# Strassen's scheme for the FFN output projections of a one-layer streaming block on Trainium2

## The chip, the cores and the metric

The kernel runs on one core of one Trainium2 chip. The metric is the device time of one execution in microseconds (us); the time of a kernel is the median of its runs. Engines are named as the profile names them: PE is TensorE, DVE is VectorE, ACT is ScalarE, SP is SyncE, whose queue issues the weight loads, and POOL is GpSimd. Each engine works through its own instruction queue in order, and semaphores tie the queues together.

## The reference

The kernel computes one layer of a post-norm block on 256 tokens of width 2048, all in float32:

```python
D_MODEL = 2048; SEQ = 256; D_FF = 5504; ALPHA = 2 ** 0.25

def swiglu_ffn(x, w_in, w_out):
    g, u = jnp.split(x @ w_in, 2, axis=-1)
    return (jax.nn.silu(g) * u) @ w_out

h = layer_norm(ALPHA * h + 0.5 * swiglu_ffn(h, ffn1_w_in, ffn1_w_out), ...)
h = layer_norm(ALPHA * h + hybrid_mixer(h, ...), ...)
h = layer_norm(ALPHA * h + memory_cross_attention(h, mem, ...), ...)
h = layer_norm(ALPHA * h + 0.5 * swiglu_ffn(h, ffn2_w_in, ffn2_w_out), ...)
```

Only the two FFNs matter here. The input projection is 256 x 2048 by 2048 x 11008 (gate and up halves of 5504 columns each), the output projection 256 x 5504 by 5504 x 2048.

## The kernel before

**Three passes for a float32 product.** TensorE multiplies in a reduced format (fp32r), so each operand is split into hi, the value rounded to that format (a CAST on ACT), and lo, the rest (a subtraction on DVE); `split` does both. A product is taken in three passes, hi·hi, lo·hi and hi·lo, which add up in a PSUM bank. Each matmul has a 128 x 128 block of activations as its stationary operand and 512 columns of weights as its moving one. The 256 tokens are two token tiles of 128.

**Loads.** Weights are read once, 1 MB at a time: a raw tile of 128 partitions x 2048 floats, from a pool of three. For the input projection a load holds two K-tiles (128 rows of the weight each) by 512 columns of the up and 512 of the gate matrix. Its two halves of 1024 columns are split into "units" (hi and lo tiles, four of each). A load is worth 2 K-tiles x 2 token tiles x 2 matrices x 3 passes = 24 matmuls. The function `run` walks a list of work items and, ahead of each, emits the DMA and the splits of loads further down the list, up to two ahead and as long as units are free; a scheduler (the Tile framework) then orders each engine's queue by the program's order, priorities (`SOON` is earlier) and its own estimate of times, and gives each tile a buffer that has come free.

**Groups.** `in_group` computes 512 gate and 512 up columns for all 256 tokens in eight loads, into four PSUM banks. `hidden` then gives two steps: `product` (silu of the gate times the up, on ACT and DVE) and `turn`, eight transposes on PE that bring the hidden block into the layout of a stationary operand, followed by a split of the turned tile from its PSUM bank (CAST on ACT, subtraction on DVE). The turn is woven in behind the second load of the next group. Banks come from two pools of four, `mm` and `at`, and consecutive groups alternate between them.

**Strassen's scheme.** Two K-tiles by two token tiles of activations are a 2 x 2 block matrix, and so are two K-tiles by two column halves of weights. In two of a group's eight loads (`SUMS_AT`, the loads 2 and 5) `mm_sums` takes the product of these by Winograd's form of Strassen's scheme: 7 block products instead of 8, hence 21 matmuls. It needs four sums of weight blocks and four of activation blocks. The weight sums are formed by `load_sums`: three additions on DVE in place in the raw tile (L177, L178), then two splits of 1024 columns into blocks that the tags X2 and X3 or H4 and H5 name. The activation sums are formed once for an FFN by `sum_forms`. Four of the seven products go into banks of the pool that the next group will use; `shared` combines them on ACT and DVE into four tiles (`w`, five buffers) that `product` adds.

**Parts and the output projection.** The hidden width is 43 K-tiles of 128. The FFN is done in three parts of 12, 16 and 15 K-tiles (`F_SPLIT`): the groups of a part, then `out_proj`, which multiplies the turned hidden tiles (blocks H0 to H3) by four K-tiles x 512 columns of output weights a load, all four column blocks in turn, plain (24 matmuls a load), and adds the bank to the residual h. The last turn of a part is woven in behind the second load of this projection.

## Time and profile before

| what | value |
| --- | --- |
| median of 3 runs | 2561.83 us (2561.34 to 2567.68) |
| profiled execution | 2568.53 us |
| its span, first to last instruction | 2566.8 us |
| granted PE clock | 0.998 |
| PE busy | 2548.4 us, 99% of the span |
| DVE busy | 1745.4 us, 68% |
| ACT busy | 1242.6 us, 48% |
| first FFN, with its layer norm | 0 to 642 us |
| mixer and cross attention | 642 to 1894 us |
| second FFN and the last layer norm | 1894 to 2567 us |

A row of the profile names the line of the kernel, the engine, the operation, the tile written and the tiles read (buffer numbers are left out), the shape, and how many instructions it stands for. In the timeline the first two numbers are the start and the duration in us, and a bracket at the end tells how long the engine was idle before it and what released it. In the table of stretches each engine has its busy time and its count of instructions; the last three numbers are the granted clock, the share of DMA time and GB/s. PEld is the load of a stationary operand, which overlaps the matmuls. T is the tile of the layer's input in its turned form, hi and lo the weight units, raw the loaded weights, X and H the blocks, w the tiles of 512 columns, ident the identity matrix of the transposes, mm and at PSUM banks.

### The profile page before, as it was taken

To read this page: it belongs to the slowest core of one execution; us is meant where nothing else is said; L and a number is where in the kernel's file an instruction comes from. 1 tells how busy PE (TensorE), PEld (TensorE's weight loads), DVE (VectorE), ACT (ScalarE), POOL (GpSimd) and SP (SyncE) were. 2 spreads that over 40 slices of the span, in tenths; PEclk is the share of its full clock that TensorE was granted. 3 is DMA by queue.
4 is the path that set the end of the run, shared out by engine and by line. 5 is a ranking of instruction groups with operands and counts; after the bars stand their busy time and mean duration, and the time that the engine had idled before them with its cause. 6 is when DMAs were issued, how large, how long until landed. Compare 5 with 4: busy or idle time off the path is not lost.

```text
span 2566.8 us, 31977 instructions
## 1 busy us (share of the span) xinstructions
PE 2548.4 (99%) x12652; PEld 2145.3 (84%) x12652; DVE 1745.4 (68%) x2317; ACT 1242.6 (48%) x1676; POOL 29.9 (1%) x87
## 2 busy tenths in 40 slices
PE   9999999999999999999999999999999999999998
PEld 8888888889888888888888888888888888888896
DVE  6857775776676776555657785555887578747856
ACT  5534553444454555544444564454554355434542
POOL 0000000000000000000000000000000000000000
PEclk9999999999999999999999999999999999999999
DMA  6655455555655642455556565543555555555563
GB/s 246 231 200 197 181 201 194 195 197 192 228 178 182 199 140 102 145 181 188 188 191 254 182 218 193 195 163 136 214 178 211 186 191 197 197 197 196 181 224 136
DMA packets 74038, 488.04 MB, mean 190 GB/s; under 512 B 8608, under 2 KB 8864, under 8 KB 20768
## 3 DMA queue, kind: packets, MB, share of 16 engines
q1 hardware_dynamic: 69216, 468.18, 50.8%
q0 software_dynamic: 3808, 15.73, 2.0%
q8 instruction: 99, 1.62, 0.2%
q10 hardware_dynamic: 864, 2.10, 0.2%
q14 instruction: 51, 0.42, 0.0%
HBM read 482.69 MB, written 2.10 MB: 189 GB/s over the span
## 4 chain that ended last, share of the span: by engine, by line
PE 95%; DVE 3%; DMA 1%; ACT 1%; issue 0%; DVEq 0%; ACTq 0%
PE mm L269 31%; PE mm L249 17%; PE mm L280 14%; PE at L280 12%; PE mm L250 8%; PE mm L325 3%; PE at L325 3%; PE mm L238 2%; PE at L814 1%; PE at L697 1%; PE at L844 1%; DVE lo L199 1%; PE at L1114 0%; DVE X L229 0%; DVE raw L178 0%; PE at L1092 0%
## 5 line engine op out<-in xcount | busy, mean ns | idle before, releaser
L199 DVE TENSOR_TENSOR lo<-raw,hi 128x1024 fp32r<-128x1024 f32 (+2 forms) x778 | 934.2, 1208 | 569.4 <-ACT hi L196 557.6
L196 ACT CAST hi<-raw 128x1024 fp32r<-128x1024 f32 (+2 forms) x778 | 807.3, 1041 | 850.9 <-PE mm L269 383.8
L269 PE MATMUL mm<-hi,H 128*128 128x512 f32 x1640 | 508.9, 390 | 1.9 <-ACT H L228 1.6
L249 PE MATMUL mm<-T,hi 128*128 128x512 f32 x1168 | 415.1, 399 | 0.0
L269 PEld LDWEIGHTS mm<-hi,H 128*128 128x128 f32 x1640 | 307.7, 188 | 66.8 <-ACT H L228 2.4
L280 PE MATMUL mm<-hi,T 128*128 128x512 f32 (+1 forms) x1152 | 347.6, 379 | 0.6 <-ACT hi L228 0.6
L250 PE MATMUL mm<-T,lo 128*128 128x256 f32 x1168 | 328.1, 281 | 0.0
L269 PE MATMUL mm<-lo,H 128*128 128x512 f32 x820 | 319.2, 389 | 0.0
L280 PE MATMUL at<-hi,T 128*128 128x512 f32 x960 | 300.4, 389 | 0.0
L249 PEld LDWEIGHTS mm<-T,hi 128*128 128x128 f32 x1168 | 219.4, 188 | 55.3 <-issue 1.5
L280 PEld LDWEIGHTS mm<-hi,T 128*128 128x128 f32 x1152 | 215.2, 188 | 36.4 <-ACT hi L228 1.2
L249 PE MATMUL mm<-H,hi 128*128 128x512 f32 x640 | 225.9, 397 | 0.0
L250 PEld LDWEIGHTS mm<-T,lo 128*128 128x128 f32 x1168 | 220.6, 189 | 0.1
L280 PE MATMUL mm<-lo,T 128*128 128x512 f32 (+1 forms) x576 | 217.8, 378 | 0.0
L280 PEld LDWEIGHTS at<-hi,T 128*128 128x128 f32 x960 | 180.2, 188 | 37.5
L280 PE MATMUL at<-lo,T 128*128 128x512 f32 x480 | 186.7, 389 | 0.0
L269 PEld LDWEIGHTS mm<-lo,H 128*128 128x128 f32 x820 | 153.9, 188 | 32.0 <-DVE lo L199 0.2
L250 PE MATMUL mm<-H,lo 128*128 128x256 f32 x640 | 179.0, 280 | 0.0
L229 DVE TENSOR_TENSOR lo<-raw,hi 128x1024 fp32r<-128x1024 f32 (+1 forms) x90 | 88.6, 987 | 107.5 <-ACT hi L228 107.5
L228 ACT CAST hi<-raw 128x1024 fp32r<-128x1024 f32 (+1 forms) x90 | 77.5, 864 | 165.4 <-PE at L280 73.0
L249 PEld LDWEIGHTS mm<-H,hi 128*128 128x128 f32 x640 | 120.2, 188 | 29.0
L269 PE MATMUL mm<-hi,X 128*128 128x512 f32 x416 | 130.5, 391 | 0.0
(230 smaller groups left out, 2911.9 us busy)
## 6 DMA issues: line engine op xcount, KB each, us to landing
raw<-ffn_w_in SPq DMA_DIRECT2D x151, 1024.0 KB, 5.0
raw<-ffn_w_out SPq DMA_DIRECT2D x80, 1024.0 KB, 4.7
raw<-w_gate SPq DMA_DIRECT2D x32, 1024.0 KB, 4.8
raw<-w_qk SPq DMA_DIRECT2D x16, 1024.0 KB, 4.8
raw<-w_o_b SPq DMA_DIRECT2D x16, 1024.0 KB, 4.8
raw<-w_out SPq DMA_DIRECT2D x16, 1024.0 KB, 4.7
raw<-w_xk SPq DMA_DIRECT2D x16, 1024.0 KB, 5.3
raw<-w_xv SPq DMA_DIRECT2D x16, 1024.0 KB, 4.7
```

The costliest lines, as they stand in the source:

```text
L196: self.nc.scalar.copy(hi[:, :m], raw[:, c:c + m])
L199: self.nc.vector.tensor_tensor(lo[:, :m], raw[:, c:c + m], hi[:, :m].bitcast(F32), ALU.subtract)
L228: self.nc.scalar.copy(hi, src)
L229: self.nc.vector.tensor_tensor(lo, src, hi.bitcast(F32), ALU.subtract)
L238: self.nc.tensor.matmul(ps, w[u][wi][:, c:c + P], x.at(xi, kt), start=(j == 0 and k == 0), stop=(j == n - 1 and k == 2),)
L249: self.nc.tensor.matmul(ps, hi, x.both(kt), start=(kt == 0), stop=False)
L250: self.last_mm = self.nc.tensor.matmul(ps[:, :S], lo, x.at(0, kt), start=False, stop=(kt == n - 1))
L269: self.last_mm = self.nc.tensor.matmul(ps, x.at(xi, kt)[:, tt * P:(tt + 1) * P], w[u][wi][:, c:c + 512], start=(start and j == 0 and k == ...
L280: self.last_mm = self.nc.tensor.matmul(ps[tt, g][:, :n], x.at(xi, kt)[:, tt * P:(tt + 1) * P], hi_lo[wi][:, g * n:(g + 1) * n], start=(kt ...
L325: self.last_mm = self.nc.tensor.matmul(bank, a[xi], hi_lo[wi][:, c:c + 512], start=own and first and j == 0, stop=own and last and j == 2)
L697: self.nc.tensor.transpose(ps[:, i * P:(i + 1) * P], s[:, c:c + P], self.ident)
L814: nc.tensor.matmul(ps[:, c0:c0 + nk], q[:, tt * P:(tt + 1) * P], k[:, :nk], start=(j == 0), stop=(j == len(parts) - 1))
```

## The change

**Two parts.** `F_SPLIT` becomes (24, 19): six groups, an output projection over 24 K-tiles, five groups (the last of three K-tiles), an output projection over 19.

**Strassen in the output projection.** `pair_group` takes the place of `in_group` and serves both projections. For the output projection `out_pair` calls it on a column half g, 1024 columns as two blocks of 512 in place of up and gate; a load is then two K-tiles x 1024 columns. At two loads of each such column half (`SUMS_OUT`: loads 3 and 8 of the first part, 3 and 6 of the second) `mm_sums` runs instead of `mm_pair`. In the first part both column halves are done so, in the second part the first one; the second half of the second part is left to `out_proj`, which reads a layout of its own. So three column halves of each FFN have two loads of 21 matmuls each. The banks alternate as between groups, `shared` combines the four banks, and its four tiles are added into h. The activation sums of each of these loads are formed while the later groups run (`forms_step`), pair by pair through two `w` tiles, into block X1; those of the input projection go into X0.

**Weight sums in a raw tile of their own, one load ahead.** `form_sums` writes the three additions into a second raw tile t (same pool of three, which now serves it too), so the loaded weights stay as they are. It is called when the load before the one with sums is emitted, so the DMA of the latter, its additions and the splits into X2 and X3 come ahead of the splits of the load before. X2 and X3 now serve every load with sums, H4 and H5 none (they hold hidden blocks). The weights are laid out accordingly on the host (`_pairs`: the blocks of a K-tile that Strassen's scheme wants exchanged).

Also, ten warm-up matmul pairs at the start become twelve. The core of the diff:

```diff
-F_SPLIT = (12, 16, 15)
-SUMS_AT = (2, 5)
+F_SPLIT = (24, 19)
+SUMS_IN = (2, 5)
+SUMS_OUT = ((3, 8), (3, 6))
+SUM_TAGS = ("X2", "X3")
...
-WARM = 10
+WARM = 12
...
+        def fetch(i):
+            if i not in raws:
+                ap = queue[i].ap if isinstance(queue[i], Sums) else queue[i][0]
+                raws[i] = self.raw_tile()
+                self.last_load = self.nc.sync.dma_start(raws[i][:, :ap.shape[1]], ap)
+            return raws[i]
+
+        def form_sums(i):
+            raw, t = fetch(i), self.raw_tile()
+            for a, b, c in ((slice(0, 1024), raw[:, 0:1024], raw[:, 512:1536]),
+                            (slice(1024, 1536), t[:, 0:512], raw[:, 1024:1536]),
+                            (slice(1536, 2048), t[:, 1024:1536], raw[:, 1536:2048])):
+                self.nc.vector.tensor_tensor(t[:, a], b, c, ALU.add)
+            sums[i] = []
+            for k in range(2):
+                blk = self.block(SUM_TAGS[k], (P, 2, 1024), F32R)
+                self.split(t[:, k * 1024:(k + 1) * 1024], blk[:, 0, :], blk[:, 1, :])
+                sums[i].append((blk[:, 0, :], blk[:, 1, :]))
+
+        def load(i):
+            w = queue[i]
+            raw = fetch(i)
+
+            for k in (i, i + 1):
+                if k < len(queue) and isinstance(queue[k], Sums) and k not in sums:
+                    form_sums(k)
...
-    def sum_forms(self, x):
+    def sum_forms(self, x, k, out):
...
+        v, f = self.w2((P, 2, S)), self.w2((P, 4, P))
+        nc.vector.tensor_tensor(v, x.blk(0, k, 2).bitcast(F32), x.blk(1, k, 2).bitcast(F32), ALU.add)
+        (a11, a21), (a12, a22) = ((v[:, i, :P], v[:, i, P:]) for i in range(2))
...
+        self.split(f, out[:, 0], out[:, 1])
...
-            main = self.collect(
-                self.out_proj, tag + "_w_out", f0, nf, lambda hid=hid: hid, half == 0,
-                st if end else None, steps if end else None, tags)
-            self.weave(main, {2: [turn]}, prio=0)
+            def out(hid=hid):
+                x = lambda: hid
+                for g in range(1 if end else 2):
+                    self.out_pair(bank ^ g, t[tag + "_w_out"][g, :, f0 * 1024:(f0 + nf) * 1024], g, nf, x, at, fh,
+                                  half == 0, st if end else None)
+                if end:
+                    self.out_proj(tag + "_w_out_r", 0, nf, x, half == 0, st, steps, tags, 2)
+            self.weave(self.collect(out), {2: [turn]}, prio=0)
...
+    def out_pair(self, bank, src, g, nk, x, at, fx, scale, st):
+
+        nc, h = self.nc, self.h
+        ps, qs = {}, {}
+
+        def shared():
+            for (tt, a), s in qs["add"].items():
+                c = (2 * g + a) * 512
+                hs = h[tt][:, c:c + 512]
+                if scale:
+                    nc.vector.scalar_tensor_tensor(hs, hs, ALPHA, s, ALU.mult, ALU.add)
+                else:
+                    nc.vector.tensor_tensor(hs, hs, s, ALU.add)
...
+        self.pair_group(bank, src, 512, nk, x, at, fx, ps, qs, shared)
+        self.add(finish)
...
-    def in_group(self, tag, j, n, xT, qs):
+    def pair_group(self, bank, src, n, nk, x, at, fx, ps, qs, then=None):
...
+            if c in at:
+                i = at.index(c)
+
+                def fn(w, i=i, c=c):
                     if i == 0:
-                        qs.update((a, self.group_tile(j + 1)) for a in range(4))
-                    self.mm_sums(ps, qs, w, xT(), self.forms, i)
-                self.add(fn, Sums(ap, (("X2", "X3"), ("H4", "H5"))[i % 2]))
-                if i == len(SUMS_AT) - 1:
+                        qs.update((a, self.group_tile(bank + 1)) for a in range(4))
+                    self.mm_sums(ps, qs, w, x(), fx["f"][:, i], 2 * c, i == 0, i == len(at) - 1)
+                self.add(fn, Sums(ap))
+                if i == len(at) - 1:
                     self.add(lambda: self.shared(qs), prio=SOON)
+                    if then:
+                        self.add(then)
                 continue
```

How the queues move is read best at the boundary between two groups. Line numbers shift: L199 of before is L215 now (the split of a load on DVE), L178 is L183 (the weight sums), L228 and L229 are L243 and L244 (the splits by `split`), L196 is L212, L280 is L296, L325 is L340, L599 to L602 are L648 to L651 (`product`), L614 is L663 (the transposes).

DVE at a boundary, before: raw_2171 is load 1 of the next group and raw_2217 its load 2, the one with sums; w_357 to w_360 are the combined tiles of the group that ends.

```order
L600 TENSOR_TENSOR w_357_2103<-w_357_2103,mm_1864 128x512
L199 TENSOR_TENSOR lo_2174<-raw_2171,hi_2173 128x1024
L599 TENSOR_TENSOR w_358_2104<-w_358_2104,mm_1865 128x512
L599 TENSOR_TENSOR w_360_2106<-w_360_2106,mm_1867 128x512
L600 TENSOR_TENSOR w_359_2105<-w_359_2105,mm_1866 128x512
L602 SCALAR_TENSOR_TENSOR w_358_2104<-w_357_2103,w_358_2104 128x512
L602 SCALAR_TENSOR_TENSOR w_360_2106<-w_359_2105,w_360_2106 128x512
L199 TENSOR_TENSOR lo_2178<-raw_2171,hi_2177 128x1024
L229 TENSOR_TENSOR lo_2220<-raw_2217,hi_2219 128x1024
L229 TENSOR_TENSOR lo_2224<-raw_2217,hi_2223 128x512
L178 TENSOR_TENSOR raw_2217<-raw_2217 128x1024
```

DVE at such a boundary, changed: raw_1112 is load 1, raw_1114 load 2 with sums, raw_1116 the extra tile.

```order
L183 TENSOR_TENSOR raw_1116<-raw_1114 128x1024
L649 TENSOR_TENSOR w_178_1044<-w_178_1044,mm_815 128x512
L648 TENSOR_TENSOR w_179_1045<-w_179_1045,mm_816 128x512
L183 TENSOR_TENSOR raw_1116<-raw_1116,raw_1114 128x512
L649 TENSOR_TENSOR w_180_1046<-w_180_1046,mm_817 128x512
L651 SCALAR_TENSOR_TENSOR w_179_1045<-w_178_1044,w_179_1045 128x512
L648 TENSOR_TENSOR w_181_1047<-w_181_1047,mm_818 128x512
...
L244 TENSOR_TENSOR X_190_1120<-raw_1116,X_190_1120 128x1024
L651 SCALAR_TENSOR_TENSOR w_181_1047<-w_180_1046,w_181_1047 128x512
L244 TENSOR_TENSOR X_191_1123<-raw_1116,X_191_1123 128x1024
L215 TENSOR_TENSOR lo_1127<-raw_1112,hi_1126 128x1024
```

The sums and both splits of the load with sums now stand between the steps of the product and ahead of the first split of load 1; before, both splits of load 1 were among the product's steps and the sums came after them. (The row left out in the second fence is the third of the three sums.)

PE at load 1 and the turn, before: hi_2177 and lo_2178 are the second unit of load 1, hi_2219 and lo_2220 the first of load 2 with sums.

```order
L280 MATMUL at_2192<-hi_2177,T_2_103 128x512
L280 MATMUL at_2192<-lo_2178,T_2_103 128x512
L280 MATMUL at_2192<-hi_2177,T_2_103 128x512
L614 MATMUL mm_2271<-ident,w_358_2104 128x128 x4
L614 MATMUL mm_2278<-ident,w_360_2106 128x128 x4
L325 MATMUL at_2189<-hi_2219,T_3_104 128x512
L325 MATMUL at_2189<-lo_2220,T_3_104 128x512
```

PE at the same place, changed: hi_1126 and lo_1127 are the first unit of load 1.

```order
L296 MATMUL at_1152<-hi_1126,T_2_103 128x512
L296 MATMUL at_1153<-hi_1126,T_2_103 128x512
L296 MATMUL at_1154<-hi_1126,T_2_103 128x512
L296 MATMUL at_1155<-hi_1126,T_2_103 128x512
L663 MATMUL mm_1223<-ident,w_179_1045 128x128 x3
L296 MATMUL at_1152<-lo_1127,T_2_103 128x512
L296 MATMUL at_1152<-hi_1126,T_2_103 128x512
L296 MATMUL at_1153<-lo_1127,T_2_103 128x512
```

The four matmuls on the hi part of load 1 are drawn ahead, three of the transposes follow, and only then the first matmul on its lo part; the other five transposes stay behind load 1.

ACT around the turn, before: hi_2262 and hi_2266 are the units of load 3, H_387 the turned tile.

```order
L228 CAST hi_2223<-raw_2217 128x512
L228 CAST X_380_2230<-raw_2217 128x1024
L196 CAST hi_2262<-raw_2260 128x1024
L228 CAST X_381_2233<-raw_2217 128x1024
L196 CAST hi_2266<-raw_2260 128x1024
L228 CAST H_387_2270<-mm_2271 128x4x128
L228 CAST H_387_2270<-mm_2278 128x4x128
```

ACT at that place, changed: hi_1214 and hi_1218 are the units of load 3, X_196 an activation sum.

```order
L243 CAST X_191_1123<-raw_1116 128x1024
L243 CAST hi_1180<-raw_1114 128x1024
L243 CAST hi_1184<-raw_1114 128x512
L243 CAST X_196_1134<-w_198_1136 128x512
L212 CAST hi_1214<-raw_1212 128x1024
L212 CAST hi_1218<-raw_1212 128x1024
L243 CAST H_212_1222<-mm_1223 128x4x128
L243 CAST H_212_1222<-mm_1230 128x4x128
```

The turned tile's casts stand behind both casts of load 3 in both kernels; the casts of the weight sums now come ahead of the plain units of the load with sums.

More of the change, by code (lines that the diff above doesn't have):

```diff
@@ L74, with __init__ @@
 class Sums:
[L79 to L80 removed]
+    def __init__(self, ap):
+        self.ap = ap
 class Kernel:
@@ new lines, in load @@
+        def load(i):
[4 more added lines that the diff above has]
+                    form_sums(k)
+            got = []
+            if isinstance(w, Sums):
+                for a, b in ((1024, 2048), (0, 512)):
+                    hi, lo = self.unit()
+                    self.split(raw[:, a:b], hi[:, :b - a], lo[:, :b - a])
+                    got.append((hi, lo))
+                return got + sums[i]
+            ap, tags = w
@@ L300, in sum_forms, with forms_step, fn, mm_sums @@
             nc.vector.tensor_tensor(f[:, j], a, b, op)
-        out = self.block("X0", (P, 2, 4, n, P), F32R)
-        self.split(tmp[:, 1, :n * 512], *(out[:, a].rearrange("p a c q -> p (a c q)") for a in range(2)))
-        return out
-    def mm_sums(self, ps, qs, w, x, forms, i):
-        k = 2 * SUMS_AT[i]
+        self.split(f, out[:, 0], out[:, 1])
+    def forms_step(self, e, tag, at, i, x):
+        def fn():
+            if i == 0:
+                e["f"] = self.block(tag, (P, len(at), 2, 4, P), F32R)
+            self.sum_forms(x(), 2 * at[i], e["f"][:, i])
+        return fn
+    def mm_sums(self, ps, qs, w, x, forms, k, first, last):
         u1, u2, t13, t24 = w
```

141 lines of the change are left out of this document (61 added, 80 removed).

## The prediction

> **What bounds the kernel now.** I read the page's first part, then its chain of waits, then a table by stage, then PE's timeline at the places that the change touches.
>
> ```profile
> span 2566.8 us, 31977 instructions
> PE 2548.4 (99%) x12652; PEld 2145.3 (84%) x12652; DVE 1745.4 (68%) x2317; ACT 1242.6 (48%) x1676; POOL 29.9 (1%) x87
> PE 95%; DVE 3%; DMA 1%; ACT 1%; issue 0%; DVEq 0%; ACTq 0%
> ...
> 0.00:642.00 642.00, 639.04 (x2887) 533.24 (x2888) 447.16 (x478) 309.04 (x351) 1.24 (x9) 1.00 0.56 203
> 642.00:1894.00 1252.00, 1250.18 (x6784) 1063.11 (x6783) 829.98 (x1320) 628.45 (x985) 27.59 (x76) 1.00 0.52 184
> 1894.00:2567.00 673.00, 659.21 (x2984) 548.98 (x2983) 468.28 (x521) 305.11 (x341) 1.07 (x2) 0.99 0.52 190
> ```
>
> TensorE is the bound in every stage: 95% of the chain, 639.0 of the first FFN's 642 us. Time goes only with matmuls or with stalls of PE. A matmul's listed duration (389 ns) overlaps the next; its price is the spacing:
>
> ```profile
> 390.56 76.20 PE mm L269 x336
> ...
> 276.29 1.36 PE mm L325 x6
> 277.65 2.72 PE at L325 x12
> 280.37 0.68 PE mm L325 x3
> ```
>
> 76.20 / 336 = 0.2268 us per matmul of 512 columns, and an undisturbed load of sums (21 matmuls, L325) takes 1.36 + 2.72 + 0.68 = 4.76 us against 24 x 0.2268 = 5.44. Stalls are of two kinds. The first is at the end of the first FFN part:
>
> ```profile
> 149.32 1.04 PE L614 MATMUL mm<-ident,w 128*128 128x128 f32 x8
> 151.15 0.50 PE L269 MATMUL mm<-hi,H 128*128 128x512 f32 x1 [0.79 <-ACT H L228]
> 151.49 0.40 PE L269 MATMUL mm<-lo,H 128*128 128x512 f32 x1
> 151.72 0.42 PE L269 MATMUL mm<-hi,H 128*128 128x512 f32 x1
> 151.98 0.40 PE L269 MATMUL mm<-lo,H 128*128 128x512 f32 x1
> 152.53 0.74 PE L269 MATMUL mm<-hi,H 128*128 128x512 f32 x2 [0.15 <-DVE H L229]
> ...
> PE mm L269 <- ACT H L228: 1.6, 2, 0.8
> ```
>
> The turned H2 is wanted at once, as the part has only three blocks. From the transposes to the fifth matmul: 152.53 - 149.32 = 3.21 us. The second kind, and the undisturbed measure of the first:
>
> ```profile
> 259.24 1.03 PE L614 MATMUL at<-ident,w 128*128 128x128 f32 x8
> 260.03 0.48 PE L325 MATMUL mm<-hi,T 128*128 128x512 f32 x1
> 260.34 0.40 PE L325 MATMUL mm<-lo,T 128*128 128x512 f32 x1
> ...
> 262.85 0.39 PE L325 MATMUL mm<-X,T 128*128 128x512 f32 x1
> 263.31 1.65 PE L325 MATMUL at<-X,X 128*128 128x512 f32 x6
> 264.79 0.62 PE L325 MATMUL mm<-X,T 128*128 128x512 f32 x2
> ...
>   DVE H L229: 6.1, 13
> ...
> 261.43 1.22 DVE L199 TENSOR_TENSOR lo<-raw,hi 128x1024 fp32r<-128x1024 f32 x1
> 262.57 1.28 DVE L229 TENSOR_TENSOR H<-at,H 128x512 fp32r<-128x512 f32 x2
> ```
>
> Undisturbed, transposes to fifth matmul is (260.03 - 259.24) + (260.34 - 260.03) + 3 x 0.2268 = 1.78 us, so the first kind costs 3.21 - 1.78 = 1.43 us; the waits list it twice, once per FFN. In the second kind the gap 262.85 to 263.31 is 0.46 instead of 0.23, and six matmuls to 264.79 take 1.48 instead of 1.36: 0.35 us, until DVE has emptied the bank of the turned tile (H<-at, which stood behind the splits). L325's own view counts 13 of these.
>
> **The change, part by part.** *Matmuls.* The order of the change has 9008 matmuls of 512 columns, that of before 9044: two pairs in each of three column pairs per FFN, three matmuls each, 2 x 3 x 2 x 3 = 36 fewer. All are on PE's path: 36 x 0.2268 = **-8.2 us**.
>
> *Two parts instead of three.* With 24 and 19 K-tiles the last turned block is wanted eight, or several, loads after its turn. Both stalls of the first kind go: 2 x 1.43 = **-2.9 us**.
>
> *Work added off PE.* Twelve more loads have sums. Each costs DVE three additions and two more splits, ACT two more casts:
>
> ```profile
> 255.43 2.68 DVE L178 TENSOR_TENSOR raw<-raw 128x1024 f32<-128x1024 f32 x3
> 258.02 1.22 DVE L229 TENSOR_TENSOR X<-raw,X 128x1024 fp32r<-128x1024 f32 x1
> ...
> L199 DVE TENSOR_TENSOR lo<-raw,hi 128x1024 fp32r<-128x1024 f32 x740 | 900.1, 1223 | 542.1 <-ACT hi L196 530.3
> L229 DVE TENSOR_TENSOR lo<-raw,hi 128x512 fp32r<-128x512 f32 x40 | 27.5, 692 | 37.0 <-ACT hi L228 37.0
> L555 DVE TENSOR_TENSOR w<-w,w 128x512 f32<-128x512 f32 x18 | 12.4, 687 | 0.0
> ```
>
> 2.6 us of sums and 1.14 us per further 1024-wide split (start to start below), some 4.5 us a load; with combining the banks and forming activation sums under 100 us of DVE in all. DVE is idle 30% of both FFNs (447 of 642), and an output stage had no such work: I cost this at nothing there. Without that cover it would be at most those 100 us, which no stage lets happen, as a load with sums has 5 to 10 us of prefetch. The extra raw tile and the single pair of X blocks matter only for when loads land: weighed now.
>
> *The boundary between groups* is where the cover is thin. There the last group's product, the next group's sums (now one load earlier) and splits meet on DVE. Before there are 14 such places; now there are 16, 14 of them with the combined product. I build the new DVE queue with the durations of one old boundary:
>
> ```profile
> 244.20 1.23 DVE L199 TENSOR_TENSOR lo<-raw,hi 128x1024 fp32r<-128x1024 f32 x1 [1.50 <-ACT hi L196]
> 246.51 0.69 DVE L600 TENSOR_TENSOR w<-w,at 128x512 f32<-128x512 f32 x1 [1.09 <-PE at L280]
> 247.12 1.22 DVE L199 TENSOR_TENSOR lo<-raw,hi 128x1024 fp32r<-128x1024 f32 x1
> 248.25 1.28 DVE L599 TENSOR_TENSOR w<-w,at 128x512 f32<-128x512 f32 x2
> ...
> raw<-ffn_w_in SPq DMA_DIRECT2D x151, 1024.0 KB, 5.0
> ...
> 248.55 1.06 ACT L196 CAST hi<-raw 128x1024 fp32r<-128x1024 f32 x1 [1.66 <-PE at L280]
> 249.51 1.15 ACT L601 ACTIVATE w<-w 128x512 f32<-128x512 f32 x2
> ```
>
> Let E be the moment the group's matmuls end, two loads before the transposes: 259.24 - 48 x 0.2268 = 248.36. The next group's load 0 is split by 245.43 = E - 2.9; the first bank is readable at E - 1.85 (L600 waited for PE). A 512-wide step takes 0.6 (247.12 - 246.51), a 1024-wide split 1.14 (248.25 - 247.12 = 1.13; 262.57 - 261.43 = 1.14), the three sums 1.3 + 0.65 + 0.65 (258.02 - 255.43 = 2.59). By the new order: first sum from E - 2.9 to -1.6; product step to -1.0; to -0.4; second sum to +0.25; three product steps to +2.05; third sum to 2.7; split X2 to 3.85; last product step to 4.45; split X3 to 5.6; then the first split of load 1, done at 6.75 to 6.85. PE begins load 1 at E + 5.44, and the new order gives it four matmuls on hi (to 6.35) and three transposes (one takes 0.11, to 6.65 or less) before the first on lo. So PE waits 0.2 to 0.3 us, 0.35 with some semaphore delay: x = 0.35.
>
> Then the turn. Splitting X3 (E + 5.7) is the last read of the extra raw tile; I take load 3 to use that tile. Landing 5.0 us after issue, it is there at E + 10.7; two casts of about 1.0 each (to 12.8), the cast of the turned tile (to 13.4); on DVE the two splits of load 3 to 14.2, the turned tile to 14.85. PE reaches the bank that waits for this at 10.88 + 8 x 0.11 + 12 x 0.2268 + 0.1 + x = 14.6 + 0.35 = 14.95: no second wait. A boundary thus costs x = 0.35 where it cost 0.35: 14 x 0.35 + 2 x 0.1 (the first groups, whose product is short) - 13 x 0.35 = **+0.5 us**. Bounds: x = 0 gives -4.6; x = 1.3, if the chain is 1 us longer, gives +13.8.
>
> *Two warm-up matmuls more* stand at the start:
>
> ```profile
> 1.07 4.64 PE L446 MATMUL at<-ones 128*128 128x128 f32 x20 [1.07 <-DVE ones L423]
> 6.35 1.74 PE L280 MATMUL mm<-hi,T 128*128 128x512 f32 x3 [0.64 <-ACT hi L228]
> ...
> 10.03 0.82 PE L280 MATMUL mm<-hi,T 128*128 128x512 f32 x2
> 10.69 0.40 PE L280 MATMUL mm<-lo,T 128*128 128x512 f32 x1
> ```
>
> 4.64 / 10 = 0.46 each, 0.9 for two, of which 0.64 was idle: at worst +0.3 us, taken as 0. Matmuls run at half speed until about 10.4 us here.
>
> The Trainium skill (page "TensorE: Matmul & The Clock Gate", Part 1, the HAM clock gate) says that full clock is granted after one free-running window of some 3.4 us was busy throughout. By that rule closing the 0.64 us of idle could bring the full clock a window earlier, and some eight matmuls would cost 0.23 instead of 0.43: the sum would be 1.6 us lower. No row here shows such a start, and the first loads may be late for it, so the sum goes without it.
>
> Sum: -8.2 - 2.9 + 0.5 = **-10.6 us**. The profiled execution took 2568.5 us (1.7 outside its span); it is 6.7 above the median of the runs, 2561.8, so a profile of the change should span about 2556, and the median should be 2561.8 - 10.6 = **2551**.
>
> **Rivals.** (A) *Both waits at the boundary go*, because sums formed ahead leave DVE free sooner than I count: x = 0, 2561.8 - 10.6 - 4.9 - 0.2 = 2546. For it: the old wait came with sums right before the turn. Against: the new queue still has 8.5 us of DVE between E - 2.9 and X3. (B) *The boundary chain is about a microsecond longer*: x = 1 adds 14 x 0.65 = 9.1: 2560, no change. For it: eleven steps without a gap, among them two that need a cast and two that need an activation. Against: ACT's rows show it idle around them (1.66 us before 248.55). (C) *Load 3 comes late and the turned tile stands behind it.* On ACT and DVE the turn's split is queued behind load 3's. If load 3 takes not the extra tile but that of load 1, which is free only at 5.6 + 2 x 1.14 = 7.9, it lands at E + 12.9 and PE waits until 17.1, 2.2 us at 14 places: +31, 2582, slower. Beyond a landing at E + 10.8 each microsecond costs 14; no gain is left from 0.75 us, and it is slower by 0.3% from 1.3 us. For it: three raw tiles now serve four uses. Against: DVE splits X3 before load 1, so the extra tile is the first one free. That the change does not take out matmuls is excluded by the order's counts.
>
> **How the numbers follow.** 0.3% (7.7 us) is about what a measurement of this kernel tells from no change. Forecast 0.50 (2551, itself 2546 to 2556; 0.08 of it within 0.3%), A 0.18, B 0.20, C 0.12. Faster 0.42 + 0.18 = 0.60; same 0.08 + 0.20 = 0.28; slower 0.12. The range reaches from A with a little for the clock, 2543, over B, to 2564, where x is 1.3; left out is most of C and the far end of A, under 0.2.
>
> **What would show it.** The PE groups of the pair matmuls: 36 fewer, at 0.227 spacing. No wait of 0.8 us at L284 or L296 on the turned block. At the boundaries: the gap before the first matmul on lo of load 1 (x), and the gap at the tenth to thirteenth matmul of load 2 (second wait); PE busy in the table by stage 10 us lower over both FFNs with the same idle. Wrong if waits of PE on "H L244" or on "lo L215" add to more than 15 us (B or C; C if load 3's cast follows a DMA), or if output stages show waits for X.

## The result

The changed kernel takes 2549.05 us (median of 6 runs, 2547.45 to 2552.43), the one before 2561.95 us (6 runs, 2561.34 to 2567.68). The ratio is 0.9948, with a 95% interval of 0.9938 to 0.9958: 13 us faster, between 11 and 16. The forecast was 2551 us, 10.6 us faster, with a range of 2543 to 2564.

The page of the changed kernel begins, with the chain's shares by engine as the last row here:

```profile
span 2546.6 us, 32083 instructions
PE 2529.7 (99%) x12620; PEld 2134.3 (84%) x12620; DVE 1824.6 (72%) x2465; ACT 1274.8 (50%) x1720; POOL 30.0 (1%) x87
...
PE 98%; DVE 1%; DMA 1%; ACT 0%; issue 0%; DVEq 0%; ACTq 0%
```

PE is busy 18.7 us less (6 of them in the middle, below). DVE is busy 79.2 us more (1745.4 to 1824.6), for the twelve further loads with sums: without them, in the first experiment, it is 1733.3. The chain is 98% PE, where it was 95%.

The spans differ by 20.2 us, the medians by 12.9. Where the rest comes from is read off the start times of two lines: the wide matmuls of the mixer and the cross attention (L249 before, L264 now) bound the middle, which the change does not touch, and the transposes of the normalised h (L376, L391) end the first FFN. (So the first FFN ends some 70 us later than 642 us, and the second begins near 1858 us, behind the last of these transposes: the limits of 642 and 1894 us in the tables ahead cut inside the FFNs.) Before, from the view of a line's instructions (the pair "A to B" is the first and last start):

```profile
L249 PE MATMUL mm<-T,hi x1168: 387/398/580, 760.6 to 1742.9; 128*128 128x512 f32 x195
L376 PE MATMUL at<-ident,h x96: 270/273/329, 709.5 to 1858.3; 128*128 128x128 f32 x96
```

And of the changed kernel:

```profile
L264 PE MATMUL mm<-T,hi x1168: 387/395/580, 752.6 to 1728.9; 128*128 128x512 f32 x195
L391 PE MATMUL at<-ident,h x96: 270/273/328, 700.5 to 1844.3; 128*128 128x128 f32 x96
```

Up to the middle 760.6 became 752.6 (-8.0); from its end to the end of the span 2566.8 - 1742.9 = 823.9 became 817.7 (-6.2). So the change is worth 14.2 us in these two profiles. The middle itself, the same instructions in the same order, took 982.3 us in the one and 976.3 in the other, and has nothing to do with the change (last section).

From PE's waits in the changed kernel (in all, times, longest):

```profile
PE mm L296 <- ACT hi L243: 1.5, 2, 0.8
...
PE mm L340 <- DVE H L244: 0.8, 1, 0.8
```

No wait on a turned block H is left in an output projection (before: 1.6 us, twice 0.8). One long wait on the turned tile stands in a load with sums (L340). At an ordinary boundary of two groups, the timeline of the changed kernel reads, for PE and then for DVE:

```profile
144.32 0.49 PE L663 MATMUL mm<-ident,w 128*128 128x128 f32 x3
144.57 0.49 PE L296 MATMUL at<-lo,T 128*128 128x512 f32 x1
144.90 0.39 PE L296 MATMUL at<-hi,T 128*128 128x512 f32 x1
...
135.07 1.23 DVE L183 TENSOR_TENSOR raw<-raw 128x1024 f32<-128x1024 f32 x1
136.21 0.68 DVE L649 TENSOR_TENSOR w<-w,mm 128x512 f32<-128x512 f32 x1
...
142.15 1.22 DVE L244 TENSOR_TENSOR X<-raw,X 128x1024 fp32r<-128x1024 f32 x1
143.29 2.35 DVE L215 TENSOR_TENSOR lo<-raw,hi 128x1024 fp32r<-128x1024 f32 x2
```

DVE's queue is the one that the prediction built, step by step, and without a gap. The first split of load 1 ends about 143.29 + 1.14 = 144.4, and PE takes its first matmul on lo at 144.57, on time. The step to the next matmul, 0.33 us instead of 0.23, is what PE takes after any transposes (0.31 at 260.03 before). It costs little: three and five transposes take 0.25 + 0.47 = 0.72 us here, where the eight at 259.24 took 0.79.

### The profile page after: what moved, and what is told of

It is laid out like the page before. It is cut to its first block, busy times and chain, and to the rows that moved or that the text cites. A ratio compares the mean times of both kernels' runs of the same rounds, so it can differ in the third digit from the quotient of the medians.

```text
span 2546.6 us, 32083 instructions
## 1 busy us (share of the span) xinstructions
PE 2529.7 (99%) x12620; PEld 2134.3 (84%) x12620; DVE 1824.6 (72%) x2465; ACT 1274.8 (50%) x1720; POOL 30.0 (1%) x87
## 4 chain that ended last, share of the span: by engine, by line
PE 98%; DVE 1%; DMA 1%; ACT 0%; issue 0%; DVEq 0%; ACTq 0%
PE at L296 20%; PE mm L296 19%; PE mm L284 19%; PE mm L264 17%; PE mm L265 8%; PE mm L340 5%; PE at L340 4%; PE mm L253 2%; PE at L865 1%; PE at L748 1%; PE at L895 1%; DMA raw<-ffn_w_in 1%; PE at L1165 0%; PE at L1143 0%; PE at L391 0%; PE mm L663 0%
## 5 line engine op out<-in xcount | busy, mean ns | idle before, releaser
L215 DVE TENSOR_TENSOR lo<-raw,hi 128x1024 fp32r<-128x1024 f32 (+1 forms) x752 | 904.3, 1210 | 569.2 <-ACT hi L212 559.6
L212 ACT CAST hi<-raw 128x1024 fp32r<-128x1024 f32 (+1 forms) x752 | 779.6, 1041 | 869.4 <-PE at L296 202.6
L264 PE MATMUL mm<-T,hi 128*128 128x512 f32 x1168 | 411.8, 397 | 0.0
L296 PE MATMUL mm<-hi,T 128*128 128x512 f32 (+1 forms) x1152 | 346.5, 377 | 1.5 <-ACT hi L243 1.5
L296 PE MATMUL at<-hi,T 128*128 128x512 f32 x960 | 300.6, 389 | 0.0
L264 PEld LDWEIGHTS mm<-T,hi 128*128 128x128 f32 x1168 | 219.2, 188 | 53.5 <-issue 1.5
L296 PEld LDWEIGHTS mm<-hi,T 128*128 128x128 f32 x1152 | 214.4, 188 | 37.0 <-ACT hi L243 2.5
L264 PE MATMUL mm<-H,hi 128*128 128x512 f32 x640 | 223.3, 394 | 0.0
L296 PE MATMUL mm<-lo,T 128*128 128x512 f32 (+1 forms) x576 | 217.9, 378 | 0.2 <-DVE lo L244 0.2
L296 PEld LDWEIGHTS at<-hi,T 128*128 128x128 f32 x960 | 180.2, 188 | 37.2
L296 PE MATMUL at<-lo,T 128*128 128x512 f32 x480 | 187.7, 391 | 0.0
L284 PE MATMUL mm<-hi,H 128*128 128x512 f32 x568 | 176.2, 389 | 0.0
L296 PE MATMUL at<-hi,H 128*128 128x512 f32 x560 | 175.0, 389 | 0.0
L264 PEld LDWEIGHTS mm<-H,hi 128*128 128x128 f32 x640 | 120.0, 188 | 27.8
L243 ACT CAST X<-raw 128x1024 fp32r<-128x1024 f32 x96 | 100.8, 1050 | 68.6 <-DVE raw L183 68.2
L243 ACT CAST hi<-raw 128x1024 fp32r<-128x1024 f32 (+1 forms) x114 | 97.1, 855 | 66.7 <-PE at L296 31.1
L284 PEld LDWEIGHTS mm<-hi,H 128*128 128x128 f32 x568 | 106.7, 188 | 22.0
L296 PEld LDWEIGHTS at<-hi,H 128*128 128x128 f32 x560 | 105.1, 188 | 21.7
```

The source lines that it names most:

```text
L212: self.nc.scalar.copy(hi[:, :m], raw[:, c:c + m])
L215: self.nc.vector.tensor_tensor(lo[:, :m], raw[:, c:c + m], hi[:, :m].bitcast(F32), ALU.subtract)
L243: self.nc.scalar.copy(hi, src)
L264: self.nc.tensor.matmul(ps, hi, x.both(kt), start=(kt == 0), stop=False)
L284: self.last_mm = self.nc.tensor.matmul(ps, x.at(xi, kt)[:, tt * P:(tt + 1) * P], w[u][wi][:, c:c + 512], start=(start and j == 0 and k == ...
L296: self.last_mm = self.nc.tensor.matmul(ps[tt, g][:, :n], x.at(xi, kt)[:, tt * P:(tt + 1) * P], hi_lo[wi][:, g * n:(g + 1) * n], start=(kt ...
```

## Experiments

Since the middle's length varies, each kernel is judged by the two stretches around it: the start of the first transposes of the normalised h, less PE's wait for them, and the time from the start of the last wide matmul to the end of the span. Repeats of one kernel agree in their sum within 0.7 us.

| kernel | first stretch | last stretch | sum | median, us | ratio to before (95%) |
| --- | --- | --- | --- | --- | --- |
| changed | 700.5 | 817.7 | 1518.2 | 2549.05 | 0.9948 (0.9938 to 0.9958) |
| changed, again | 703.3 - 2.9 | 817.6 | 1518.0 | 2553.34 | 0.9953 (0.9938 to 0.9968) |
| plain output pairs | 704.4 | 821.6 | 1526.0 | 2562.11 | 0.9985 (0.9975 to 0.9995) |
| the same, three parts | 705.5 | 821.9 | 1527.4 | 2561.42 | 0.9984 (0.9975 to 0.9994) |
| sums late | 699.3 | 816.2 | 1515.5 | 2552.12 | 0.9953 (0.9942 to 0.9965) |
| sums late, again | 701.4 - 1.9 | 816.7 | 1516.2 | 2553.21 | 0.9954 (0.9940 to 0.9969) |
| sums late and in place | 704.9 - 2.9 | 818.6 | 1520.6 | 2551.85 | 0.9958 (0.9943 to 0.9973) |
| a sum taken twice | 705.6 - 1.7 | 818.6 | 1522.5 | 2556.18 | 0.9970 (0.9956 to 0.9985) |
| sums late, three in a group | 697.2 - 1.4 | 816.7 | 1512.5 | 2550.82 | 0.9943 (0.9927 to 0.9958) |
| sums late, no early w_va | 699.4 | 816.2 | 1515.6 | 2552.82 | 0.9945 (0.9931 to 0.9959) |
| ten warm-up pairs | 702.6 - 2.3 | 816.7 | 1517.0 | one run | |

The medians of this table depend on which of the two lengths of the middle each kernel happened to draw, and do not rank kernels a few us apart; the sums do.

### Plain output pairs

```diff
-SUMS_OUT = ((3, 8), (3, 6))
+SUMS_OUT = ((), ())
```

(With it the factor on h is applied when the banks are added.)

> The changed kernel without Strassen's scheme in the output projections: all their loads are plain pairs of 24 matmuls, with two parts, early sums and all else kept. Count theory: the 36 matmuls of 512 columns come back, 36 x 0.2268 = 8.2 us, and nothing else moves, so 2549 + 8.2 = 2557, about 5 us under the kernel before; in the profile no wait of PE comes or goes in the output stages. Rival (the sums there cost something off the count, on DVE or in late loads): the saving was less than the count, so it comes back as 5 us or less, 2554 or below. Rival (sums in the output relieve something, fewer hi/lo units wanted for instance): 10 us or more, 2559 or above.

Its span is 2560.3 us, and these two lines mark the stretches:

```profile
L264 PE MATMUL mm<-T,hi x1168: 387/398/580, 756.4 to 1738.7; 128*128 128x512 f32 x195
L391 PE MATMUL at<-ident,h x96: 270/273/329, 704.4 to 1854.2; 128*128 128x128 f32 x96
```

The two stretches grow by 3.9 us each, 7.9 in all, where the count says 18 x 0.2268 = 4.1 each. The saving is the matmuls, and the work that the output's sums put on DVE is hidden. (The median fell among the runs with the long middle; its runs with the short one, 2555.1 to 2556.3, are 8 us above the changed kernel's.)

### The same in three parts

```diff
-F_SPLIT = (24, 19)
+F_SPLIT = (12, 16, 15)
-SUMS_OUT = ((3, 8), (3, 6))
+SUMS_OUT = ((), (), ())
```

> As the run with plain output pairs, but in three parts of 12, 16 and 15 K-tiles as before. Predicted step: the stall of 1.43 us at the end of the first part of each FFN comes from the part being short, so it returns: 2.9 us above the run with plain output pairs, with waits of 0.8 us of PE on the cast of the turned block H. Rival (the layout): a load of the output pairs holds two K-tiles by 1024 columns, where the loads of before held four K-tiles by 512, so the third turned block is wanted only at the fifth load, two loads (10.9 us) after its turn, also in a part of 12: the stall stays away, the time is that of the run with plain output pairs within 1 us, and two parts alone are worth nothing.

PE at the end of the first part of the first FFN:

```profile
148.80 1.03 PE L663 MATMUL mm<-ident,w 128*128 128x128 f32 x8
149.59 0.48 PE L296 MATMUL at<-hi,H 128*128 128x512 f32 x1
149.90 0.40 PE L296 MATMUL at<-lo,H 128*128 128x512 f32 x1
```

After the turn of the part's last block PE goes on in step: no stall, though the part has twelve K-tiles as before. The sum is 1.4 us above that with two parts, none of it here. Of that 1.1 us is the measure: in three parts the trace has five more matmuls ahead of the first transposes of the normalised h (2882 of 512 columns, 2877 in two parts), and the first wide matmul of the middle starts at 756.5 and 756.4. The other 0.3 stands at the second FFN's first group, below. So the stall of 1.43 us was removed by the layout: a load of the output pairs holds two K-tiles, and the block just turned is first wanted two loads later; before, a load held four K-tiles and the third one began with that block. The rival holds, and the number of parts alone is worth at most some 0.4 us.

### Sums with their own load

```diff
-            for k in (i, i + 1):
+            for k in (i,):
```

> The changed kernel with the weight sums formed with their own load, not one load ahead; the extra raw tile stays. PE's queue then has all eight transposes behind load 1 again and its passes in the plain order. Theory 1 (forming ahead removed the old wait): DVE's splits of X2 and X3 stand just before the turned tile's again, PE waits some 0.35 us in the load with sums at 14 boundaries where it now waits 0.12: 3 us more, 2552. Theory 2 (the old wait came from the sums in place, which have to wait for the plain splits of the same raw tile, and from what stood between X3 and the turned tile): by the queue's order and the durations of the boundary, X3 is split by 10.3 us after the end of the group's matmuls, load 2's plain units by 12, load 3's by 13.5 and the turned tile by 14.5, wanted at 14.6: no wait beyond 0.1 us, and no wait at load 1 either: 2548 to 2549.

PE's waits, of the first run of this kernel, in full up to the smallest:

```profile
PE mm L296 <- ACT hi L243: 1.2, 1, 1.2
PE at L461 <- DVE ones L438: 1.1, 1, 1.1
PE at L895 <- ACT w L754: 0.8, 5, 0.2
PE mm L296 <- DVE lo L244: 0.2, 1, 0.2
```

No wait is left at any boundary, nor at the second FFN's first group, and the sum falls by 2.7 us (in a repeat, below, 0.2 us is left at that group). Theory 2 holds and more: forming the sums one load ahead, which the change does, costs it some 2.2 us (1518.1 against 1515.9, means of two profiles each; some 0.8 of it at the second FFN's first group). DVE and PE at the boundary of this kernel show why nothing is late:

```profile
145.68 1.21 DVE L244 TENSOR_TENSOR X<-raw,X 128x1024 fp32r<-128x1024 f32 x1
146.81 1.81 DVE L244 TENSOR_TENSOR lo<-raw,hi 128x1024 fp32r<-128x1024 f32 x2
...
151.17 1.28 DVE L244 TENSOR_TENSOR H<-mm,H 128x512 fp32r<-128x512 f32 x2
...
148.69 1.03 PE L663 MATMUL mm<-ident,w 128*128 128x128 f32 x8
```

X3 is split by 146.9, the plain units by 148.6, and the turned tile by 151.17 + 1.28 = 152.4, in time for the matmuls on its bank. All eight transposes stand together again.

The same kernel beside a repeat of the change:

> The kernel with the sums formed with their own load, once more beside the changed kernel, since the times of its first runs were all in the slower of the two groups that the middle stages make. By its FFN stages (750.2 and 802.9 us against 751.5 and 804.8) it is 3.2 us faster than the change: groups at 2546 and 2552. Rival: the slower middle comes with this kernel, and it stays at 2552, no faster than the change.

Its sum repeats (1516.2). Its times, 2546.9 to 2556.4, overlap those of the change, 2548.1 to 2558.4, since the middle's 6 us and a wait at the layer norm (below) lie over both; no version was shown faster than the change by its median.

### Late and in place

```diff
-            raw, t = fetch(i), self.raw_tile()
+            raw = t = fetch(i)
```

(The sums are formed after the plain splits of the same tile.)

> As the kernel with late sums, but the sums are formed in place in the raw tile, after its plain splits, as before the change; X2 and X3 still serve every load with sums, and there is no extra raw tile. On DVE the plain splits of the load with sums come first, the sums after them, and between X2 and X3 stands the next load's split. Theory (the old wait comes from the sums in place): X3 and so the turned tile are as late as in the kernel before, 14.2 us after the end of the group's matmuls for the start of its split, and PE waits 0.35 us at 14 boundaries: the FFN stages take 4.9 us more than with late sums in a tile of their own, 1558 us in all instead of 1553. Rival (the extra tile is not what matters, but the alternation of the blocks, or the output's plain loads in two parts): no wait, 1553.

A load with sums in it:

```profile
196.18 0.39 PE L340 MATMUL mm<-X,T 128*128 128x512 f32 x1
196.60 1.65 PE L340 MATMUL at<-X,X 128*128 128x512 f32 x6
```

The step from 196.18 to 196.60 is 0.42 us instead of 0.23, the old second kind of wait, at nearly every boundary again, and the sum is 4.7 us above that of late sums with their own tile (5.1 against its first profile; 4.9 expected). So that wait came from the sums being formed in place, which puts them after the plain splits, and it is the raw tile of its own that removes it.

### One sum taken twice

```diff
                             (slice(1536, 2048), t[:, 1024:1536], raw[:, 1536:2048])):
+                            (slice(1536, 2048), t[:, 1024:1536], raw[:, 1536:2048])):
```

> The changed kernel with the third of the weight sums taken twice (the same result): 0.6 us more of DVE in each of 48 loads with sums, 28 us in all. The order that comes with it puts both splits of load 1 ahead of X3's, leaves all eight transposes behind load 1, gives load 3 the raw tile of load 1 and puts the turned tile's split ahead of load 3's. Edge theory (DVE's queue at the boundary has no slack, so each added step is paid there): 14 x 0.55 = 8 us more, 2557. Order theory (what counts is what stands ahead of load 1's first split; by the durations it is done 5.95 us after the end of the group's matmuls and wanted at 6.12, the turned tile long before 14.6): no wait at any boundary, 14 x 0.1 and the 0.9 us at the second FFN's first group saved, 2546 to 2548 in spite of the added work.

Neither: at ten of fourteen boundaries PE does not wait, at four it waits 0.6 to 1.4 us for the first split of load 1. DVE ahead of the worst one but one:

```profile
136.75 1.23 DVE L184 TENSOR_TENSOR raw<-raw 128x1024 f32<-128x1024 f32 x1 [1.21 <-DMA raw<-ffn_w_in]
...
143.82 0.68 DVE L184 TENSOR_TENSOR raw<-raw,raw 128x512 f32<-128x512 f32 x1
144.43 2.35 DVE L216 TENSOR_TENSOR lo<-raw,hi 128x1024 fp32r<-128x1024 f32 x2
```

The first sum of load 2, at the head of the boundary's chain, waited 1.2 us for its DMA, and the eleven steps behind it, with the split of load 1 among them, shifted as one. At the other three of the four it waited 0.7 to 0.9 us for its DMA as well, at the ten without a wait of PE not at all. With sums formed ahead, the boundary depends on the arrival of a load that PE wants only two loads later; both theories took load 2 as landed.

### Three pairs in each input group, sums late

```diff
-SUMS_IN = (2, 5)
+SUMS_IN = (2, 4, 6)
```

(The pools of the `w` tiles and of the small tiles beside them are cut to four buffers to make room.)

> The kernel with late sums and three pairs by Strassen's scheme in each group of the input projection (loads 2, 4 and 6) instead of two; to make room for the larger block of activation sums the two small pools are cut from 5 and 6 buffers to 4 each. 54 matmuls fewer over both FFNs: 54 x 0.2268 = 12.2 us less than with late sums, and DVE gets 18 loads x 4.5 = 81 us more work. Count theory: PE bounds, FFN stages 1553.1 - 12.2 = 1541, some 13 to 15 us below the change. Rival (the last sums are now one load, 5.4 us, ahead of the group's end, and the four combining steps on DVE push the product and so the turn back): half a microsecond or more at each of 18 boundaries, and with fewer buffers waits in the middle stages: the gain is cut to 3 us or less.

54 matmuls fewer bring 3.0 us instead of 12.2; the middle takes 2 us more. Waits of the turned tile come back, the longest at the second FFN's first group:

```profile
1905.06 1.91 PE L340 MATMUL mm<-X,X 128*128 128x512 f32 x6 [2.85 <-DVE H L244]
1906.77 0.63 PE L296 MATMUL at<-hi,T 128*128 128x512 f32 x1
1907.19 0.63 PE L296 MATMUL at<-lo,T 128*128 128x512 f32 x1
...
1909.73 0.39 PE L296 MATMUL at<-lo,T 128*128 128x512 f32 x1
```

After 2.85 us of idleness PE also ran eight matmuls at half speed (0.43 us from start to start). Rival: the cover is used up, and fewer buffers cost in the middle. Which of the two edits brought back which wait was not separated.

### The change again, and ten warm-up pairs

> The changed kernel once more, unaltered, as the yardstick for what one profile of it tells. From the first matmul to the middle stages and from these to the end its first profile took 751.5 and 804.8 us, and the middle stages 976.6, where those of before and of the other runs so far took 982.5 with the same instructions. If the middle has two lengths at random, this profile has one of the two, the FFN stages repeat within 1 us, and the times fall into two groups some 6 us apart (2548 and 2554). If the length of the middle goes with the kernel, it is 976.6 again and there is one group.

The middle took 982.0 us this time, so its length does not go with the kernel. The stretches repeat (1518.0). But PE waited 2.9 us for the layer norm at the end of the first FFN:

```profile
PE at L391 <- DVE h L383: 2.9, 1, 2.9
```

The view of DMA issues around this place (the last number is the median from issue to landing), and DVE's timeline:

```profile
raw<-w_va SPq DMA_DIRECT2D x6, 1024.0 KB, 6.9
```

```profile
693.71 2.36 DVE L215 TENSOR_TENSOR lo<-raw,hi 128x1024 fp32r<-128x1024 f32 x2 [3.39 <-ACT hi L212]
696.38 2.36 DVE L215 TENSOR_TENSOR H<-raw,H 128x1024 fp32r<-128x1024 f32 x2 [0.31 <-ACT H L212]
698.66 0.68 DVE L674 TENSOR_TENSOR h<-h,mm 128x512 f32<-128x512 f32 x1
```

The mixer's first weights landed 6.9 us after their issue (4.8 in the first profile of the change). DVE's last addition to h stands behind the splits of three of these loads (that into H is the third) and the layer norm behind the addition. In the kernel before, the third load's splits came after the addition; its w_va also took 6.9 us in the profile, and yet PE waited less (its waits, and the DMA issues):

```profile
PE at L376 <- DVE h L368: 0.8, 1, 0.8
```

```profile
raw<-w_va SPq DMA_DIRECT2D x4, 1024.0 KB, 6.9
```

So the change also moved a load ahead of the layer norm, which costs nothing when w_va is on time and 2 to 3 us of waiting, and 1.7 more until the middle, when it is late; the 1.7 are matmuls at half speed after the wait (last section).

```diff
-WARM = 12
+WARM = 10
```

> The changed kernel with ten warm-up pairs as before. With twelve, the first matmuls come at full speed from 7.3 us on (0.23 us each), where before they took 0.43 us each until 10.4, and yet the stream from the first group's end on starts only 0.25 to 0.35 us earlier, since the second load's hi part is late (a gap of 1.1 us at 9.2). Clock theory: with ten pairs the half speed until about 10.4 us is back and the stream starts 0.3 us later, at 8.4 instead of 8.1 (time of the 190th matmul less 190 spacings). Rival (loads alone set the start): no difference over 0.1 us.

```profile
1.07 4.64 PE L461 MATMUL at<-ones 128*128 128x128 f32 x20 [1.07 <-DVE ones L438]
6.47 1.25 PE L296 MATMUL mm<-hi,T 128*128 128x512 f32 x3 [0.76 <-ACT hi L243]
7.56 0.39 PE L296 MATMUL mm<-lo,T 128*128 128x512 f32 x1
7.79 0.39 PE L296 MATMUL mm<-hi,T 128*128 128x512 f32 x1
```

With ten pairs full speed came at 7.5 us too, after an idle time of 0.76 us that is longer than the 0.64 of before, and the stream starts at 8.15, where the two profiles of the change have 8.2 and 8.1. The clock theory falls: twelve pairs are worth nothing here, and the half speed until 10.4 us in the profile of before does not come from there being ten. This fits what the Trainium skill says of the clock gate (page "TensorE: Matmul & The Clock Gate", Part 1), that its window runs freely and its phase varies between runs. That it was the phase is not shown: there is one profile of before.

### No early third load at the layer norm

```diff
-            (None, None, ("H5", "H0", "early"), ("X0", "X1"))))
+            (None, None, ("H5", "H0"), ("X0", "X1"))))
```

> The kernel with late sums, with one more edit at the end of the first FFN: the mixer's third load (w_va, split into blocks H5 and H0) is not fetched early, so its two splits no longer stand ahead of the last addition and the layer norm on DVE. Two profiles of the change differ there: where the w_va loads landed 4.8 us after their issue PE waited 0.2 us for the layer norm, where they landed after 6.9 us it waited 2.9 us, and the stretch around it took 4.7 us longer. Theory (the late split stands in the way): no wait of PE on the normalised h above 0.5 us even where w_va lands late, and the times lose the group some 4.6 us above the fastest; 2546 and 2552 by the two lengths of the middle. Rival (the third load is now late for the mixer's first matmuls): PE waits there for two or three us instead, and nothing is gained. Rival (the layer norm waits for the first two w_va loads, whose splits stay ahead of it): the wait is the same.

> The kernel with late sums and the mixer's third load not fetched early, once more, for a profile in which w_va lands late: in its first profile the loads landed after 4.9 us and the question did not arise. If w_va takes 6 us or more here, theory (the third load's splits stand in the way): PE waits less than 1 us for the layer norm, where it waited 1.9 to 2.9 us in the late profiles of the other kernels; rival (the splits of the first two loads, which stay ahead of the layer norm, are late too): 1.5 us or more. If it takes about 5 us, this run says nothing on it but adds times.

> The same kernel and the same question as the run before it, for a second chance of a profile with a late w_va: below 1 us of waiting for the layer norm by the theory, 1.5 us or more by the rival.

PE's waits and the DMA issues of the third profile, the one with the latest w_va of the three (4.9, 5.1 and 6.1 us):

```profile
PE mm L284 <- DVE H L215: 0.5, 1, 0.5
PE at L391 <- DVE h L383: 0.3, 1, 0.3
```

```profile
raw<-w_va SPq DMA_DIRECT2D x5, 1024.0 KB, 6.1
```

PE did not wait for the layer norm of the first token tile in any of the three, where the late profiles of the other kernels wait. It waited 0.3 us for that of the second, and 0.5 us for the late third load. How the load acts is read off its landing. In all six profiles that have this wait with the third load early (1.4 to 2.9 us), the first transposes begin 8.04 to 8.05 us after the third w_va load has landed: at 703.3 after 695.3 in the repeat of the change, at 701.4 after 693.4 in that of late sums. (From the second load it is 10.5 to 11.9.) In the third profile of this kernel the third load landed at 692.7, which would have put them at 700.8; they began at 699.5, without a wait. So it is the third load that stood in the way, and without it there the wait is gone. The 14 times of this kernel lie at 2547.5 to 2548.9 and 2552.6 to 2553.8, none above, where the 12 of the change reach 2558.4 (in a profile with that wait and the long middle) and the 11 of late sums 2556.4. That fits the theory too; what PE would wait with w_va as late as 6.9 us, no profile shows. By time this kernel is not told from the change: 2548.0 and 2548.3 in its second and third set, 2549.05 for the change.

## Why the prediction was right

The time fell inside the range, 2 us below the forecast, and the sign was right. Term by term, against 14.2 us in the two profiles:

- **Matmuls, -8.2.** Right: taking them back cost 7.9 us.
- **Part ends, -2.9.** Right in size, wrong in cause. The step "with 24 and 19 K-tiles the last turned block is wanted eight, or several, loads after its turn" names the parts; with parts of 12 the stall stayed away too. It was the pair layout, which I had read in the diff and not followed to the turn.
- **The boundary, +0.5.** Wrong by 2.8 us. The queue was built rightly, but its durations were a little too high: the first sum's step was put at 1.3 us and took 136.21 - 135.07 = 1.14, the chain to the end of load 1's first split at 9.65 and took 144.43 - 135.07 = 9.36, and so the split ended just in time. Rival A (x = 0, the waits go) is what happened at ordinary boundaries. Beside it stand some 1.0 us at one place, 0.2 at two others, and some 0.3 in all for transposes taken in two lots. The 13 old waits were not all of 0.35 us either: by the starts of PE's matmuls they are 0.26 to 0.35, in all 4.1 where the sum has 13 x 0.35 = 4.55. They became about 1.8: -2.3.
- **Rival C** happened once, at the second FFN's first group, where the product is short and the sums' chain differs:

```profile
1891.11 2.00 ACT L212 CAST hi<-raw 128x1024 fp32r<-128x1024 f32 x2 [4.57 <-DMA raw<-ffn_w_in]
1893.01 1.06 ACT L243 CAST H<-mm 128x512 fp32r<-128x512 f32 x2
...
1892.19 2.36 DVE L215 TENSOR_TENSOR lo<-raw,hi 128x1024 fp32r<-128x1024 f32 x2 [3.07 <-ACT hi L212]
1894.47 1.28 DVE L244 TENSOR_TENSOR H<-mm,H 128x512 fp32r<-128x512 f32 x2
```

  Load 3's cast waits for its DMA, and the turned tile's cast and split are queued behind, as the rival had it; PE loses 1.0 us once and not 2.2 at 14 places: at the ordinary boundary above ACT casts load 3 from 148.30 on, without a wait for its DMA. The loss is not fixed: 0.9 us in the repeat of the change, 0.1 with ten warm-up pairs.
- **The start, 0.** 0.3 us were gained against the profile of before, where PE ran at half speed until 10.4 us, and not by the two pairs.
- **Not in the sum:** the layer norm at the end of the first FFN. The sum has no term for it; its work is the same, but the order on DVE just ahead of it moved. In the first pair of profiles it gained the 0.8 us that PE waited before, in the late ones it loses 2 to 3.

Together -7.9 - 2.9 - 2.3 - 0.8 - 0.3 = -14.2, as the two profiles have it. That it closes to the tenth is partly chance: by the starts of PE's matmuls the part ends give 3.0 and the layer norm 1.2, and some 0.5 us of small steps elsewhere stand against them unexplained. The forecast was 3.6 us short of that sum. It came near because the two terms that carry it, matmuls and part ends, had the right size; one of these had the wrong reason, and what the boundary and the layer norm gained was left out. That the median came within 2 us of the forecast is in part luck: the two fastest runs, 2547.5 and 2548.1, lie about as far below it as the profiles say, and three runs at 2549.7 to 2552.4, none of them profiled, moved the median back.

## What to carry to other kernels

Work formed ahead of need is not free on an engine with one queue: it puts the arrival of a later load at the head of the chain that the next load needs, and here a tile of its own removed the old wait while forming early gave half of the gain back. When a stall disappears, follow the consumer: here it was the order in which a new layout wants its blocks, not the longer part. And compare kernels a few us apart by stretches that repeat, not by medians over something that varies between executions.

## What the runs showed of the hardware

The middle has two lengths, 6 us apart, in executions of one and the same program. One stretch of 100 us of the changed kernel, and then of its repeat, in the table by stretch:

```profile
1100.00:1200.00 100.00, 100.00 (x579) 87.47 (x578) 59.52 (x77) 49.09 (x73) 0.00 (x0) 1.00 0.53 185
```

```profile
1100.00:1200.00 100.00, 100.00 (x567) 86.76 (x567) 58.86 (x77) 47.71 (x71) 0.00 (x0) 1.00 0.53 189
```

PE never idles, the granted clock is 1.00, and yet 579 or 567 of the same matmuls go through in 100 us, 2% apart, for some 320 us. Of 14 profiles three had the short form, and the runs' times fall into two groups accordingly (2561.6 and 2567.7 for the kernel before). What sets it was not found.

Loads of w_va landed after 4.8 or 6.9 us at the same place of the same program. In the semaphore events of the late profile 15 of the 16 parts of the second such load had arrived by 690.1 us and the last at 692.5. Why one part lags in some executions stays open.

A wait of PE of about 2 us was enough for a spell at half speed. The twelve matmuls behind the first transposes of the normalised h, in the repeat of the change (a wait of 2.9 us just before) and in its first profile (no wait):

```profile
704.16 4.59 PE L284 MATMUL mm<-X,H 128*128 128x512 f32 x12
```

```profile
701.33 3.01 PE L284 MATMUL mm<-X,H 128*128 128x512 f32 x12
```

In the first of them eight matmuls, from 704.75 on, start 0.43 us apart instead of 0.23: that is most of the 1.7 us. All five profiles in which PE waited 1.9 to 2.9 us at one place have such a spell, of 3.4 to 3.5 us, which begins with the first instruction after the wait or up to 1.3 us later. Waits of 1.4 and 1.7 us, in two profiles, were followed by none.
